# Split operand tiles and right-hand pools on multiples of 64 bytes in a hybrid DeltaNet / gMLP / MLP step

## The chip, the cores and the metric

The kernel runs on one core of a Trainium2 chip. The metric is the device time of one execution in microseconds. A core has a tensor engine (PE, with its weight loads shown apart as PEld), a vector engine (DVE), a scalar engine (ACT), GpSimd (POOL) and a sync engine (SP) whose queue issues the transfers here. Tiles live in SBUF, 128 partitions; a tile's address is a byte offset that is the same in every partition.

## The reference

One layer of a backbone is computed for 128 context tokens and 2048 latent tokens, width 1024. Per token tile:

```
h = rmsnorm(x) * (1 + sc1) + sh1
q, k, v, gate, ab, u, vg = split(h @ w_in)           # q, k, v through a 3-wide convolution and silu
o_a = gated DeltaNet of q, k, v, both directions, chunks of 64, 4 heads x 128
o_b = gelu(u) * (spatial mix of layernorm(gelu(vg)) in chunks of 128)
x = x + ga1 * (concat(rmsnorm(o_a) * silu(gate), o_b) @ w_out)
h = rmsnorm(x) * (1 + sc2) + sh2
x = x + ga2 * (square(relu(h @ w_ff1)) @ w_ff2)       # width 4096
y = rmsnorm(x)
```

The outputs are y of both sequences and the context's final DeltaNet states.

## The kernel before

Every large product is made of three products of operands split into a high and a low part: `mm3` (L213) issues high x high (L217), high x low (L218) and low x high (L219) into the same PSUM tile. The high part is a tile of type fp32r, the low part what is left. Tokens stand in 17 tiles of 128.

*First phase.* Six blocks (`BLOCKS`, L28), five of three token tiles and one of two, are normalised and modulated. `column(k)` (L448) makes the split operands of slice k of the width: `kH` and `kL`, two tiles of 388 columns of 4 bytes from the tag `h`, 24 buffers in the pool `p1`. Block 0 uses 388 columns of them, blocks 1 to 4 use 386 (384 and a neighbour at each end), the last 258. They are streamed through PE (`pj<-kH,wH` and its like): 12 feature tiles (4 each of k, q and v) of 8 slices for each block. At the ends stand single columns, which POOL copies in, zeros from `zcol`.

*Scan.* Then come 34 units of the DeltaNet scan, one for each token tile and direction, beside the gate, gMLP and output projections. A unit prepares a triangular inverse in 16-bit tiles (`AH`, `X`, `Y`, `R` and others) and 32-bit ones (`KK`, `E`, `Es`), which lie in the pool `prep` at the right side of SBUF. When the last unit is prepared, `swap_right` (L1329) closes that pool and opens `hopA` in its place.

*MLP.* Both matmuls use a scheme of seven block products in place of eight (`ORDER`, L54). What PE streams here is a `hop` tile: 4 slices of K, a high and a low part of 512 columns each, 16384 bytes per partition.

```
side, bufs = ("A", 2) if n else ("B", 5)                      # hop_tile, L893
hop[g, o] = t = hop_tile(F32R, o in ORDER[:2])                # first matmul, L900
moved.append(hop_tile(F32R, (len(tcount) - 1) % 5 < 2))       # second matmul, L1630
```

In the first matmul the hop tiles hold the token operands of the seven products for one of two groups of tokens; products 1 and 5 (the first two of `ORDER`) take a tile of `hopA`, the others one of `hopB`. A unit is a pair of 128 columns of the first weight; there are 16 units for each group, and for each product of a unit the four slices of the hop tile are used once: 12 products on PE. In the second matmul the hop tiles hold the second weight, four tiles for each of the seven products, in turn two from `hopA` and three from `hopB`. Its loop (L1757 to the end) runs over `(product, u, q)`: 9 or 8 units u for each product (9, 8, 8, 9, 9, 8, 9), and for each four visits q, one on each hop tile, 12 products each.

*Addresses.* A pool on the left side follows those opened before it, one with `side="right"` grows down from the right end. Tiles are rounded up to 32 bytes. The right end here is byte 229344, 32 more than a multiple of 64. So before the change `hopA` has its two tiles at bytes 196576 and 212960, and all tiles of `prep` lie 32 above a multiple of 64. The five tiles of `hopB` lie on multiples of 64 (from 113024 to 178560), and so do the 49 tiles of `wp`, where the weights and z operands lie. The buffers of `kH` and `kL` are 1568 bytes apart, so every second one is 32 off. A column gives its `kH` and its `kL` neighbouring buffers, so one of the two is off and the other not.

The order of the instructions is set by a scheduler when the program is built, from the order written and dependences. The step from the first phase to the scan reuses addresses: the right pool `prep` takes those where the first phase's `cv`, `x2`, `tk` and `kTt` (pool `p1f`) lay.

Of the kernel before, what the change touches and what calls it, by code (L numbers as in the profile page):

```python
# [8 lines left out]
F32 = mybir.dt.float32  # L9
F32R = mybir.dt.float32r  # L10
# [7 lines left out]
P = 128  # L18
D = 1024
KT = D // P  # L20
# [41 lines left out]
def hybrid_step(  # L62
# [11 lines left out]
    def xrow(t):  # L74
        return x_prompt[0] if t == 0 else x_sample[0, (t - 1) * P : t * P, :]
# [7 lines left out]
    def f32(ap):  # L83
        return ap.bitcast(F32)

    cp = ctx.enter_context(tc.tile_pool(name="const", bufs=1))
    dp = ctx.enter_context(tc.tile_pool(name="dram", bufs=1, space=DRAM))


# [23 lines left out]
    make_identity(nc, ident)  # L113
    ident16 = cp.tile([P, P], F16, name="ident16")
    V.tensor_copy(ident16, ident)
    nhalf = cp.tile([P, 72], F32, name="nhalf")
    V.memset(nhalf, -0.5)
    zcol = cp.tile([P, KT], F32, name="zcol")
    V.memset(zcol, 0.0)
    bd2 = cp.tile([P, P], F16, name="bd2")  # L120
    om = {w: cp.tile([P, P], F16, name=f"om{w}") for w in (2, 4, 8, 16, 32)}
# [50 lines left out]
    def rsqrt_cols(out, ss, n, scale, eps):  # L172
        t = smp.tile([P, 72], F32, tag="rsq", name="rsq", bufs=2)
        np_ = ss.shape[0]
        V.tensor_scalar(out=t[:np_, :n], in0=ss, scalar1=scale, scalar2=eps, op0=ALU.mult, op1=ALU.add)  # L175
        G.tensor_tensor(out=out, in0=t[:np_, :n], in1=nhalf[:np_, :n], op=ALU.pow)  # L176
# [83 lines left out]
    with ExitStack() as ph:  # L260
        p1 = ph.enter_context(tc.tile_pool(name="p1", bufs=2, reuse_waits="tile"))
# [7 lines left out]
        def pt():  # L269
            return ppt.tile([P, 512], F32, tag="pt", name="pt", bufs=3)  # L270
# [121 lines left out]
        def prep_block(bi):  # L392

            tiles = BLOCKS[bi]
            n = len(tiles) * P
            if bi == 0:
                ncol, segs = 388, [(1, 0, P, 0), (131, P, 2 * P, 1)]
            else:
                ncol, segs = n + 2, [(1, 0, n, 1)]
            hH, hL = [], []  # L400
            c0 = tiles[0] * P
            xs = []

            def load_x(t):
                if bi == 0:
                    xs.append(xs0[t])
                    return
                x = p1.tile([P, D], F32, tag="x", name="x", bufs=3)
                load(out=x, in_=xrow(t))
                if t == tiles[0]:  # L410
                    xs.append(smp.tile([P, 3], F32, tag="ss3", name="xss"))
                i = t - tiles[0]
                junk = p1.tile([P, D], BF16, tag="junk", name="junk", bufs=1)
                A.activation(junk, x, AF.Square, accum_out=xs[0][:, i : i + 1])

            def columns_r():
                nt = len(tiles)
                r = smp.tile([P, 3], F32, tag="rk", name="xr")
                rsqrt_cols(r[:, :nt], xs[0][:, :nt], nt, 1.0 / D, EPS)
                diag = p1.tile([P, 3, P], F32, tag="diag", name="diag", bufs=1)  # L420
                V.tensor_tensor(out=diag[:, :nt, :], in0=ident.unsqueeze(1).to_broadcast([P, nt, P]),
                                in1=r[:, :nt].unsqueeze(2).to_broadcast([P, nt, P]), op=ALU.mult)
                xs.append(diag)

            def rows_r():

                pr = pt()
                T.matmul(pr[:, :n], ones, xs[1][:, : len(tiles), :].rearrange("p a b -> p (a b)"), start=True,
                         stop=True)
                xs[1] = p1.tile([P, 384], F32, tag="rrow", name="rrow", bufs=1)  # L430
                A.copy(xs[1][:, :n], pr[:, :n])

            pairs = []

            def load_pair(j):
                x = p1.tile([P, D], F32, tag="x", name="xT", bufs=3)
                x = x[:, : 2 * n].rearrange("p (k t) -> p k t", k=2)
                load(out=x, in_=x_columns.rearrange("(k p) t -> p k t", p=P)[:, 2 * j : 2 * j + 2, c0 - P : c0 - P + n])
                pairs.append(x)

            zc, hc = [], []
            if bi == 0:
                zc, hc = [0, 129, 130], [(387, 1)]
            elif bi == 5:
                zc, hc = [n + 1], [(0, 8)]
            else:
                hc = [(0, 2 * bi - 2), (n + 1, 2 * bi + 1)]
            def column(k):  # L448
                full = p1.tile([P, 384], F32, tag="full", name="full", bufs=2)
                kH = p1.tile([P, 388], F32R, tag="h", name="kH", bufs=24)  # L450
                kL = p1.tile([P, 388], F32R, tag="h", name="kL", bufs=24)
                for col in zc:
                    G.tensor_copy(kH[:, col : col + 1], zcol[:, 0:1])
                    G.tensor_copy(kL[:, col : col + 1], zcol[:, 0:1])
                for col, j in hc:
                    G.tensor_copy(kH[:, col : col + 1], f32(halH)[:, k, j : j + 1])
                    G.tensor_copy(kL[:, col : col + 1], f32(halL)[:, k, j : j + 1])
                if bi == 0:
                    ps = pt()
                    for i, x in enumerate(xs):  # L460
                        T.transpose(ps[:, i * P : (i + 1) * P], x[:, k * P : (k + 1) * P], ident)
                    for s, o, m, cd in segs:
                        A.activation(full[:, o : o + m], ps[:, o : o + m], AF.Identity,
                                     scale=a1[:, cd, k : k + 1], bias=b1[:, cd, k : k + 1])
                    for s, o, m, _ in segs:
                        V.tensor_copy(kH[:, s : s + m], full[:, o : o + m])  # L466
                        V.tensor_tensor(out=kL[:, s : s + m], in0=full[:, o : o + m], in1=f32(kH)[:, s : s + m],
                                        op=ALU.subtract)
                else:
                    if k == 2:  # L470
                        load_pair(3)
                    b = b1[:, 1, k : k + 1]
                    V.scalar_tensor_tensor(out=full[:, :n], in0=pairs[k // 2][:, k % 2, :], scalar=a1[:, 1, k : k + 1],
                                           in1=xs[1][:, :n], op0=ALU.mult, op1=ALU.mult)
                    A.activation(kH[:, 1 : n + 1], full[:, :n], AF.Identity, bias=b)
                    V.scalar_tensor_tensor(out=kL[:, 1 : n + 1], in0=full[:, :n], scalar=b,
                                           in1=f32(kH)[:, 1 : n + 1], op0=ALU.add, op1=ALU.subtract)
                for s, o, m, _ in segs:
                    store(out=hH_d[:, k, c0 + o : c0 + o + m], in_=f32(kH)[:, s : s + m])
                    store(out=hL_d[:, k, c0 + o : c0 + o + m], in_=f32(kL)[:, s : s + m])  # L480
                hH.append(kH)
                hL.append(kL)
            blk = (hH, hL, ncol, segs)
            first = [lambda t=t: load_x(t) for t in tiles]
            if bi:
                first += [lambda: (columns_r(), load_pair(0)), lambda: (rows_r(), load_pair(1)), lambda: load_pair(2)]
            return blk, first, [lambda k=k: column(k) for k in range(KT)]

        def feature_tile(blk, bi, gi, h):
# [249 lines left out]
        side = []  # L739
        for bi in range(len(BLOCKS)):  # L740
# [8 lines left out]
            for n, (gi, h) in enumerate(order):  # L749
# [40 lines left out]
                side = []  # L790
# [114 lines left out]
    with ExitStack() as ph:  # L905
        right = ctx.enter_context(ExitStack())
# [945 lines left out]
    for m, (n, i, u, q) in enumerate(todo):  # L1852
# [12 lines left out]
        h, lo = sops.pop(m)  # L1865
# [72 lines left out]
```

## Time and profile before

| What | Value |
|---|---|
| runs | 2718.88, 2714.51, 2715.29 us; median 2715.29 |
| span of the profiled execution, first to last instruction | 2715.6 us |
| its own time beside the span | not given apart from the runs; the span is 0.3 us over the median |
| granted clock of PE | 0.990 of full speed, mean |
| PE busy | 2631.7 us, 97% |
| DVE, ACT, POOL busy | 1867.8, 1247.8, 226.4 us |
| HBM read, written | 398.14, 179.74 MB |

PE's rows are read by their starts: products overlap in the engine, and the end of each is modelled, so that the time from one start to the next says how fast they follow each other. In a row of the timeline stand start, duration, engine, line, operation, what is written, what is read (the streamed operand first, the stationary one behind it), rows x columns of the stationary operand, and the shape streamed. The names carry no buffer numbers: which hop tile a row reads follows from its place in the loop.

### The profile page before, as it was taken

The page shows a single profiled execution, that of the slowest core. Times are in us where ns is not written, and L with a number is a line of the kernel's source. Part 1 is how long each engine was busy: PE and PEld are TensorE (multiplying, and loading weights), DVE is VectorE, ACT ScalarE, POOL GpSimd, SP SyncE. Part 2 cuts the span into 40 slices and gives each one's busy share as a digit, 9 for nine tenths or more (in the row PEclk, how much of TensorE's full clock was granted, in tenths as well). Part 3 has the DMA queues.
Part 4 walks back from the last instruction along what each step waited for, and adds up shares of the span by engine and source line. Part 5 has one row for each costly group of instructions (what it writes and reads, how often), then busy time and mean ns, then how long its engine had stood idle before and what let it go on. Part 6 is the DMA issues. An engine that isn't in the chain of part 4 may idle for free.

```text
span 2715.6 us, 45142 instructions
## 1 busy us (share of the span) xinstructions
PE 2631.7 (97%) x15682; PEld 2195.9 (81%) x15682; DVE 1867.8 (69%) x3911; ACT 1247.8 (46%) x3092; POOL 226.4 (8%) x448
## 2 busy tenths in 40 slices
PE   8999999999999999899999999999999999999998
PEld 4999998787887777778888778888888787788887
DVE  5867655877777879885677857665565556775874
ACT  4655555555555567763355533332342432332441
POOL 3112113111111111110000000000000000000000
PEclk9999999999999989999999999999999999999999
DMA  8867539555555657885877796333459978776782
GB/s 293 281 198 223 184 119 293 170 159 152 165 160 167 196 174 244 276 271 179 286 222 231 212 311 206 111 110 106 122 166 364 336 257 300 272 240 215 231 262 90
DMA packets 569387, 580.91 MB, mean 214 GB/s; under 512 B 35692, under 2 KB 401692, under 8 KB 565574
## 3 DMA queue, kind: packets, MB, share of 16 engines
q1 hardware_dynamic: 569158, 578.03, 66.9%
q8 instruction: 123, 2.02, 0.3%
q14 instruction: 106, 0.87, 0.1%
HBM read 398.14 MB, written 179.74 MB: 213 GB/s over the span
## 4 chain that ended last, share of the span: by engine, by line
PE 82%; DMA 7%; DVE 6%; issue 2%; ACT 1%; SPq 1%; POOL 0%; DVEq 0%; POOLq 0%; ACTq 0%
PE f L219 16%; PE f L217 16%; PE f L218 16%; PE pj L217 6%; PE pj L219 6%; PE pj L218 6%; PE pd L952 2%; DMA qT<-qT_d 2%; PE pm L217 1%; PE pm L219 1%; PE pm L218 1%; PE pd L1131 1%; DMA raw<-in_w_mod_dram 1%; PE pd L1132 1%; PE pt L568 1%
## 5 line engine op out<-in xcount | busy, mean ns | idle before, releaser
L219 PE MATMUL f<-hop,zL 128*128 128x512 f32 x960 | 377.6, 394 | 1.7 <-DVE zL L1450 1.7
L217 PE MATMUL f<-hop,zH 128*128 128x512 f32 x960 | 377.4, 393 | 1.7 <-ACT zH L1456 1.7
L218 PE MATMUL f<-hop,zH 128*128 128x512 f32 x960 | 377.5, 394 | 0.0
L217 PE MATMUL f<-hop,wH 128*128 128x512 f32 x896 | 356.2, 398 | 6.1 <-ACT wH L1456 6.1
L218 PE MATMUL f<-hop,wH 128*128 128x512 f32 x896 | 352.2, 393 | 0.0
L219 PE MATMUL f<-hop,wL 128*128 128x512 f32 x896 | 352.1, 394 | 0.0
L1456 ACT CAST zH<-zraw 128x512 fp32r<-128x512 f32 x240 | 147.0, 620 | 291.3 <-DVE zraw L1450 90.8
L217 PEld LDWEIGHTS f<-hop,zH 128*128 128x128 f32 x960 | 180.6, 188 | 45.4 <-ACT zH L1456 3.4
L219 PEld LDWEIGHTS f<-hop,zL 128*128 128x128 f32 x960 | 180.7, 188 | 45.0 <-DVE zL L1450 3.5
L218 PEld LDWEIGHTS f<-hop,zH 128*128 128x128 f32 x960 | 180.7, 188 | 41.1
L1450 DVE TENSOR_TENSOR zL<-zraw,zH 128x512 fp32r<-128x512 f32 x240 | 162.6, 686 | 67.9 <-ACT zH L1456 52.6
L217 PEld LDWEIGHTS f<-hop,wH 128*128 128x128 f32 x896 | 169.6, 189 | 41.3 <-ACT wH L1456 6.5
L219 PEld LDWEIGHTS f<-hop,wL 128*128 128x128 f32 x896 | 169.2, 189 | 38.1 <-DVE wL L1450 0.3
L218 PEld LDWEIGHTS f<-hop,wH 128*128 128x128 f32 x896 | 169.4, 189 | 35.4
L217 PE MATMUL pj<-kH,wH 128*128 128x386 f32 (+2 forms) x568 | 190.6, 338 | 0.6 <-DVE kH L466 0.3
L219 PE MATMUL pj<-kH,wL 128*128 128x386 f32 (+2 forms) x568 | 190.3, 335 | 0.0
L218 PE MATMUL pj<-kL,wH 128*128 128x386 f32 (+2 forms) x568 | 189.5, 334 | 0.0
L176 POOL TENSOR_TENSOR r<-rsq,nhalf 128x1 f32<-128x1 f32 (+1 forms) x38 | 23.1, 607 | 1520.8 <-DVE rsq L175 1520.8
L516 DVE SCALAR_TENSOR_TENSOR cv<-pj,vec,cv 128x384 f32<-128x384 f32 (+2 forms) x164 | 87.1, 539 | 60.4 <-ACT cv L513 56.5
L1450 DVE TENSOR_TENSOR wL<-raw,wH 128x512 fp32r<-128x512 f32 x112 | 76.1, 687 | 76.3 <-ACT wH L1456 75.3
L217 PEld LDWEIGHTS pj<-kH,wH 128*128 128x128 f32 x568 | 107.2, 189 | 5.2 <-issue 4.7
L218 PEld LDWEIGHTS pj<-kL,wH 128*128 128x128 f32 x568 | 107.5, 189 | 0.5
(404 smaller groups left out, 6083.0 us busy)
## 6 DMA issues: line engine op xcount, KB each, us to landing
zraw<-z_d SPq DMA_DIRECT2D x212, 256.0 KB
raw<-in_w_ff_dram SPq DMA_DIRECT2D x128, 256.0 KB
hop<-hop_d SPq DMA_DIRECT2D x28, 1024.0 KB
z_d<-c SPq DMA_DIRECT2D x96, 256.0 KB
zraw<-s_d SPq DMA_DIRECT2D x96, 256.0 KB
raw<-in_w_mod_dram SPq DMA_DIRECT2D x80, 256.0 KB
r<-in_w_ff_dram SPq DMA_DIRECT2D x80, 256.0 KB
s_d<-s SPq DMA_DIRECT2D x64, 256.0 KB
```

What stands on the lines that cost most here:

```text
L176: G.tensor_tensor(out=out, in0=t[:np_, :n], in1=nhalf[:np_, :n], op=ALU.pow)
L217: T.matmul(ps, lh, rh, start=first and i == 0, stop=False, skip_group_check=more)
L218: T.matmul(ps, lh, rl, start=False, stop=False, skip_group_check=more)
L219: T.matmul(ps, ll, rh, start=False, stop=last and i == n - 1, skip_group_check=more)
L516: V.scalar_tensor_tensor(out=cv[:, o : o + m], in0=ps[:, s + sh : s + sh + m], scalar=convw[:, w, j : j + 1], in1=cv[:, o : o + m], op0=AL ...
L568: T.matmul(ps[:, i * P : (i + 1) * P], kTt[:, i * P : (i + 1) * P], rhs[:, i * P : (i + 1) * P], start=True, stop=True)
L952: T.matmul(p[:, h, :], lhs[:, h, :], rhs[:, h, :], start=True, stop=True)
L1131: T.matmul(p[:, h, :], u["qT"][:, h, :], s[:, h, :], start=True, stop=False)
L1132: T.matmul(p[:, h, :], u["QK"][:, h, :], u["vn"][:, h, :], start=s is None, stop=True)
L1450: V.tensor_tensor(out=out, in0=a, in1=b, op=op)
L1456: A.copy(h, src)
```

## The change

A pool `edge` is opened first at the right side, and `zcol` (32 bytes) moves into it, so that everything else at the right side lies 32 bytes lower. `nhalf` grows by the 32 bytes that `zcol` leaves free, so the tiles behind both keep their addresses. `kH` and `kL` get 400 columns, a stride of 1600 bytes; the columns that are used stay the same. Afterwards `hopA` lies at bytes 196544 and 212928, the tiles of `prep` on multiples of 64, all 24 buffers of `kH` and `kL` too; what lies above them in `p1` and `p1f` is 768 bytes higher than before.

```
     cp = ctx.enter_context(tc.tile_pool(name="const", bufs=1))
+    edge = ctx.enter_context(tc.tile_pool(name="edge", bufs=1, side="right"))
...
-    nhalf = cp.tile([P, 72], F32, name="nhalf")
+    nhalf = cp.tile([P, 80], F32, name="nhalf")
     V.memset(nhalf, -0.5)
-    zcol = cp.tile([P, KT], F32, name="zcol")
+    zcol = edge.tile([P, KT], F32, name="zcol")
...
-                kH = p1.tile([P, 388], F32R, tag="h", name="kH", bufs=24)
-                kL = p1.tile([P, 388], F32R, tag="h", name="kL", bufs=24)
+                kH = p1.tile([P, 400], F32R, tag="h", name="kH", bufs=24)
+                kL = p1.tile([P, 400], F32R, tag="h", name="kL", bufs=24)
```

The instructions of every engine and their order are the same before and after.

## The prediction

> **What bounds the kernel now.** I read the page's busy times, clock row and chain first, then the costliest groups, then the timeline of PE (the tensor engine), because a change of addresses can act only through the time of single instructions.
>
> ```profile
> span 2715.6 us, 45142 instructions
> PE 2631.7 (97%) x15682; PEld 2195.9 (81%) x15682; DVE 1867.8 (69%) x3911; ACT 1247.8 (46%) x3092; POOL 226.4 (8%) x448
> PEclk9999999999999989999999999999999999999999
> PE 82%; DMA 7%; DVE 6%; issue 2%; ACT 1%; SPq 1%; POOL 0%; DVEq 0%; POOLq 0%; ACTq 0%
> L219 PE MATMUL f<-hop,zL 128*128 128x512 f32 x960 | 377.6, 394 | 1.7 <-DVE zL L1450 1.7
> L217 PE MATMUL f<-hop,wH 128*128 128x512 f32 x896 | 356.2, 398 | 6.1 <-ACT wH L1456 6.1
> ```
>
> PE is busy for 97% of the span and 82% of the chain that ended last. The two last rows stand for the MLP: its 5568 products (3 x 960 + 3 x 896) stream a `hop` tile of 512 columns and wait for other engines for some us in all. So what changes the spacing of PE's instructions changes the time. The mean of 394 to 398 ns is a modelled duration and mixes all tiles; the spacing must be read from starts.
>
> The built programs before and after have the same instructions in the same order on every engine; only addresses and a few waits where the scan follows the first phase differ. Before, the right end of SBUF lies 32 bytes off a multiple of 64, so the two `hopA` tiles start at bytes 196576 and 212960 of a partition, both 32 above a multiple of 64; the five `hopB` tiles start on multiples of 64. In the second matmul of the MLP a visit is 12 products (four slices of K, three products each) on one hop tile, and four visits make one unit. In its first product the tiles of the visits are A, A, B, B. PE's timeline, each row the first L217 of a visit (start, duration):
>
> ```profile
> 2043.16 0.40 PE L217 MATMUL f<-hop,zH 128*128 128x512 f32 x1
> ...
> 2045.97 0.39 PE L217 MATMUL f<-hop,zH 128*128 128x512 f32 x1
> ...
> 2048.77 0.40 PE L217 MATMUL f<-hop,zH 128*128 128x512 f32 x1
> ...
> 2051.53 0.39 PE L217 MATMUL f<-hop,zH 128*128 128x512 f32 x1
> ...
> 2054.25 0.40 PE L217 MATMUL f<-hop,zH 128*128 128x512 f32 x1
> ```
>
> The two A visits take 2.81 and 2.80 us, the B visit after them 2.76, the second B visit 2.72, and no row between has an idle time. 2.72 / 12 = 226.7 ns per product on B, 2.80 / 12 = 233.3 on A. An A visit costs 0.08 to 0.09 us more, and the B visit behind it another 0.04 until the spacing has settled.
>
> **The change part by part.** No edit has a time of its own: `nhalf` has 8 more columns in the one memset that fills it at the start; the pool `edge` holds only `zcol`; `kH` and `kL` are allocated 400 wide, but every instruction on them keeps its 258, 386 or 388 columns. What they bring is addresses: `hopA` and the scan's preparation tiles (same right side) move down by 32 bytes onto multiples of 64, and the split tiles of the first phase, every second of which lay 32 off (stride 1568 bytes, now 1600), all lie on multiples of 64.
>
> *The hop tiles.* Count of A visits: the first matmul has 32 units (16 column pairs, two groups of tokens) and A holds the operands of products 1 and 5: 64 visits. In the second, tile k of the running count is A when k mod 5 is 0 or 1: two visits of four in the products of 9, 8, 8, 8 and 9 units, one in those of 9 and 9, so 2 x 42 + 18 = 102. Together 166 visits, 1992 products. If A runs like B, 166 x 0.085 = 14.1 us go. The after-effect: 60 units of the second matmul x 0.04 = 2.4 us; in the first some 30 more places, but there single products of the context tile lie between and restart the pattern anyway, so I take half, 0.6. Sum 17.1 us; ends 0 (the alignment is not what makes A slow) and 14.9 + 2.4 + 1.2 = 18.5 (0.09 for each visit).
>
> *The split tiles of the first phase.* Here both kinds alternate in one stretch. Rows of the first phase: from 335.69 four triples with `kH` 32 off and `kL` not (8 of 12 products off), then four with `kL` 32 off and `kH` not (4 of 12 off).
>
> ```profile
> 335.69 0.34 PE L217 MATMUL pj<-kH,wH 128*128 128x386 f32 x1
> ...
> 337.83 0.34 PE L217 MATMUL pj<-kH,wH 128*128 128x386 f32 x1
> ...
> 339.96 0.34 PE L217 MATMUL pj<-kH,wH 128*128 128x386 f32 x1
> ...
> 418.67 0.28 PE L217 MATMUL pj<-kH,wH 128*128 128x258 f32 x1
> ...
> 419.75 0.28 PE L217 MATMUL pj<-kH,wH 128*128 128x258 f32 x1
> ```
>
> 2.14 and 2.13 us per 12. What 12 aligned ones would take no row shows. The last two rows hold 9 products of 258 columns in 1.08 us, 120 ns each; with 226.7 for 512 columns that is 0.42 ns per further column, so 386 columns would take 226.7 - 126 x 0.42 = 173.8 ns and 12 of them 2.085 us. The excess is 0.05 us per 12. There are 12 feature tiles x 8 slices x 5 blocks = 480 triples of 386 or 388 columns, so 120 such groups: 6.0 us at most. The least is 0: the two groups differ by 0.01 us only, the products of 258 columns are two thirds off and show no excess over the line through them, and part of the 0.05 can be the ripple behind the transposes that cut in every few products. I take the middle, 3.0 us. PE has nothing else to wait for there:
>
> ```profile
> core 0: us, PE busy (x) PEld busy (x) DVE busy (x) ACT busy (x) POOL busy (x), PEclk, DMA share, GB/s
> 200.00:400.00 200.00, 200.00 (x1233) 190.40 (x1232) 127.97 (x250) 105.83 (x328) 33.94 (x96) 1.00 0.56 174
> 800.00:1000.00 200.00, 182.29 (x1538) 149.00 (x1537) 156.49 (x434) 112.24 (x312) 27.03 (x33) 0.95 0.58 178
> 2040.00:2143.00 103.00, 101.81 (x440) 82.23 (x439) 59.36 (x90) 36.71 (x64) 0.00 (x0) 1.00 0.99 355
> 2143.00:2232.00 89.00, 89.00 (x387) 72.37 (x386) 40.93 (x63) 33.50 (x58) 0.00 (x0) 1.00 0.86 299
> ```
>
> *What takes some back.* DMA, 0.99 busy at 355 GB/s from 2040 to 2143 (the product that also builds the sums of the weights). Nine units there would gain 9 x 0.21 = 1.9 us; if the transfers cannot come faster, PE waits instead. I take 1.0 lost, ends 0 and 1.9. From 2143 on the share is 0.86 and less, DVE 40.93 of 89 us: nobody is late there for a 1% faster PE. If one is, it is the split of z (`zH`, then `zL`), which PE waits on for 1.7 us in all now.
>
> *The scan's preparation tiles.* I cost their move at nothing, from rows of both kinds of address (before the change `R`, `X` and `E` are 32 off; `ident16`, `QK`, `x` and `tmp` are not):
>
> ```profile
> L1084 PE MATMUL pd<-R,X 128*128 128x128 f16 x136 | 13.3, 220 | 0.0
> L1003 PE MATMUL pd<-ident,X 128*128 128x128 f16 x136 | 13.5, 223 | 0.0
> L1044 DVE TENSOR_TENSOR QK<-QK,E 128x512 f32<-128x512 f32 x34 | 23.3, 687 | 19.3 <-DMA QK<-qk_d 12.6 <-POOL E L982 5.4 <-DMA gate_d<-th 1.2
> L1319 DVE TENSOR_TENSOR x<-x,tmp 128x512 f32<-128x512 f32 x34 | 23.3, 686 | 0.5
> ```
>
> A 16-bit product that streams `R` takes 220 ns, one that streams `ident16` 223; DVE with `E` 687, without 686. The stage has slack as well (PE 182.29 of 200).
>
> *The waits where the scan begins.* With the pool edges moved by 768 bytes below and 32 above, the first two units' `KK` and `E` wait for other last users of the phase before; the first load of `KK` waits for one store less, the next load of `hL` for one more. In the chain there:
>
> ```profile
> 447.31 5.14 DMA vt_d<-tk
> ...
> 464.97 2.85 POOL KK L992
> ```
>
> I cost it at 0 with ends of 2.85 us either way, one such step.
>
> Sum: 17.1 + 3.0 - 1.0 = 19.1 us. Against the profiled execution's span, 2715.6 - 19.1 = 2696.5. The median of the three runs is 2715.29, 0.3 less, so I say 2696. From the ends of the terms: least gain with the mechanism right 13.3 + 2.4 + 0 - 1.9 - 2.85 = 11.0 (166 x 0.08 = 13.3), most 18.5 + 6.0 + 2.85 = 27.4.
>
> **The rivals.** *A is slow for another reason than its 32 bytes.* `hopA` is also the highest part of SBUF, and the after-effect shows in aligned B tiles, so place and alignment are not told apart by the MLP's rows. Then `hopA` stays at 2.80, at most the first phase gains, and the time is 2715.6 - 3.0 = 2712.6, no change that can be told. For it: no run has an A tile on a multiple of 64. Against it: 6.7 ns more per product on every A product, in both matmuls of the MLP, is what a fixed number of extra columns at the start or end of a stream would cost (0.42 ns per column: 16 columns, 64 bytes), as an extra piece read per stream would; and `R` above lies higher still, at byte 228320, without a price, though as a 16-bit stream it needs half the bytes.
>
> The Trainium skill bears on this rival: SBUF — State Buffer, section "Door 1: The DMA port swizzle", says that SBUF is read in lines of 16 bytes and that a price comes with each crossing to a new line. By that rule a row of 2048 bytes that starts at a multiple of 32 covers the same 128 lines wherever it starts, no term above would be there, and the time would stay 2715.6. The trace has 2.80 against 2.72 us for rows of the same length, which that rule does not give, but its tiles differ in place as well.
>
> *DMA eats half.* If the weight and z streams set the pace in more than one product, about half of the second matmul's 102 visits come to nothing: 102 x 0.085 / 2 = 4.3, and half of its after-effect, 1.2; 2696.5 + 5.5 = 2702. For it the 0.99 row, against it the 89.00 of 89.00 us busy in the row below.
>
> *Slower.* Before, the preparation tiles and the scan's own tiles lie on different halves of 64 bytes; if equal halves make engines block each other, each of the scan's 170 levels (34 units, five levels: 680 products in groups of four) gets longer on its way PE, DVE, PE. To turn 19 us of gain into more than 5 us of loss the 170 levels must lengthen by 24.5 / 170 = 0.14 us each; with 0.18 it gives 2696.5 + 30.6 = 2727. Against it: the DVE rows above, 687 with tiles on both halves, 686 on one.
>
> **How the numbers follow.** 0.2% is 5.4 us, about what a measurement of this kernel can tell from no change. Forecast (A runs like B) 0.78, DMA takes half 0.07, A slow by place 0.12, slower 0.03. So faster 0.85, same 0.12, slower 0.03. The forecast's own range is 2688 (most gain, 27.4) to 2704.6 (least, 11.0). A range for 8 in 10 reaches from 2688 over both first cases and a part of the third, to 2710.
>
> **What would show it.** Right: four equal visits of 2.72 us per unit in the second matmul; 12 products of 386 columns in 2.09 to 2.11 us; the 16-bit rows and DVE rows as above; the MLP shorter by 16 us and the first phase by 3. Wrong: A visits still of 2.80 (the place, not the alignment); A visits of 2.72 but new idle time of PE before L217 for `zH` (DMA or the split); a first POOL `KK` later than 464.97 less the first phase's gain; longer scan levels.

## The result, and the profile after

| Kernel | runs | median us | lowest to highest | ratio to before, 95% interval |
|---|---|---|---|---|
| before, beside it | 5 | 2715.29 | 2712.76 to 2718.88 | |
| changed | 5 | 2705.08 | 2703.27 to 2710.52 | 0.9962 [0.9951, 0.9974] |

The change makes the kernel 10.2 us faster, by the interval 7.1 to 13.3. That is about half of the 19.1 us that the prediction summed up. The profiled execution of the changed kernel was the slowest of its five (2710.52 us), so its profile shows a smaller gain, 6.9 us of span. In all kernels from here on the three products stand one line lower: L218, L219 and L220. The page of the changed kernel, in the places that were quoted before:

```profile
span 2708.8 us, 45143 instructions
PE 2625.1 (97%) x15682; PEld 2196.0 (81%) x15682; DVE 1867.8 (69%) x3911; ACT 1246.7 (46%) x3092; POOL 226.4 (8%) x448
PE 79%; DMA 8%; DVE 8%; ACT 2%; issue 2%; SPq 1%; POOL 0%; DVEq 0%; POOLq 0%; ACTq 0%
L220 PE MATMUL f<-hop,zL 128*128 128x512 f32 x960 | 377.0, 393 | 1.8 <-DVE zL L1451 1.7
L218 PE MATMUL f<-hop,wH 128*128 128x512 f32 x896 | 356.0, 398 | 7.0 <-ACT wH L1457 7.0
```

PE is 6.6 us less busy, DVE and POOL are as before, and the waits ahead of the products are within 1 us of the old ones: the gain is spacing of products. The mean of one product in the rows shown (393 and 398 ns, before 394 and 398) hardly shows it, as the prediction warned. Its size is in the starts of the visits, on PE's timeline in the same unit of the second matmul (visits A, A, B, B, and the next unit's A):

```profile
2038.58 0.40 PE L218 MATMUL f<-hop,zH 128*128 128x512 f32 x1
...
2041.34 0.40 PE L218 MATMUL f<-hop,zH 128*128 128x512 f32 x1
...
2044.09 0.40 PE L218 MATMUL f<-hop,zH 128*128 128x512 f32 x1
...
2046.86 0.39 PE L218 MATMUL f<-hop,zH 128*128 128x512 f32 x1
...
2049.58 0.40 PE L218 MATMUL f<-hop,zH 128*128 128x512 f32 x1
```

2.76, 2.75, 2.77 and 2.72 us, where before stood 2.81, 2.80, 2.76 and 2.72. The unit is 11.00 us long and was 11.09. A visits became faster, but they did not become like B, and the first B visit behind them even lost 0.01.

The second matmul by stretches, in the windows of before and then of the changed kernel: its first product, the second and third together, and the fourth.

```profile
2032.03:2133.61 101.58, 100.39 (x435) 81.04 (x435) 55.00 (x84) 34.42 (x60) 0.00 (x0) 1.00 1.00 354
2133.61:2313.35 179.74, 179.74 (x774) 144.33 (x773) 101.33 (x158) 58.31 (x100) 0.00 (x0) 1.00 0.86 291
2313.35:2419.09 105.74, 103.47 (x437) 82.12 (x436) 75.45 (x123) 33.04 (x57) 0.00 (x0) 0.98 0.74 247
```

```profile
2027.55:2129.22 101.67, 100.05 (x435) 80.92 (x434) 54.78 (x84) 34.35 (x60) 0.00 (x0) 1.00 0.99 351
2129.22:2307.43 178.21, 178.21 (x774) 144.41 (x772) 100.54 (x156) 57.26 (x98) 0.00 (x0) 1.00 0.85 291
2307.43:2414.21 106.78, 103.86 (x438) 81.51 (x436) 76.83 (x125) 34.43 (x59) 0.00 (x0) 0.98 0.75 250
```

The first numbers are the stretch, its length and PE's busy time; the last three are PE's clock, the share of the DMA engines and GB/s. Where PE is busy all the time (the middle row), 16 units got 1.53 us shorter. In the first product PE's busy time fell by 0.34 us and its length did not: the idle time grew from 1.19 to 1.62 us, with the DMA engines at 0.99. In the fourth both PE's busy time and its idle time are larger than before.

From first to last start, the first matmul went from 727.03 to 724.31 us (-2.7), the second from 674.54 to 672.15 (-2.4), the first phase from 391.1 to 391.5 (+0.4) and the stretch between the two, which holds the scan, from 869.2 to 869.3 (+0.1). Over the 14 profiles of this case the first phase scatters from 391.1 to 394.9 us and the scan's stretch from 864.6 to 870.8, so that one profile does not show a change of 1 us there. The 2.3 us that remain lie ahead of the first phase's first product. That first stretch is 43.2 us long in the profile of before, 43.3 in that of `cols386` (below) and 40.0 to 41.7 in all others. `cols386` and `cols384` have the addresses of before, and `cols384` has 40.4, so nothing ties this length to the change.

### The profile page after: what moved, and what is told of

It reads as the page before. It is cut to its first block, busy times and chain, and to the rows that moved or that the text cites. A ratio compares the mean times of both kernels' runs of the same rounds, so it can differ in the third digit from the quotient of the medians.

```text
span 2708.8 us, 45143 instructions
## 1 busy us (share of the span) xinstructions
PE 2625.1 (97%) x15682; PEld 2196.0 (81%) x15682; DVE 1867.8 (69%) x3911; ACT 1246.7 (46%) x3092; POOL 226.4 (8%) x448
## 3 DMA queue, kind: packets, MB, share of 16 engines
HBM read 398.14 MB, written 179.74 MB: 213 GB/s over the span
## 4 chain that ended last, share of the span: by engine, by line
PE 79%; DMA 8%; DVE 8%; ACT 2%; issue 2%; SPq 1%; POOL 0%; DVEq 0%; POOLq 0%; ACTq 0%
PE f L218 16%; PE f L220 16%; PE f L219 15%; PE pj L218 6%; PE pj L220 5%; PE pj L219 5%; PE pd L953 2%; DMA qT<-qT_d 1%; PE pm L218 1%; PE pm L315 1%; PE pm L219 1%; PE pm L220 1%; DMA QK<-qk_d 1%; PE pd L1132 1%; PE pt L569 1%
## 5 line engine op out<-in xcount | busy, mean ns | idle before, releaser
L218 PE MATMUL f<-hop,zH 128*128 128x512 f32 x960 | 378.2, 394 | 2.7 <-ACT zH L1457 2.7
L220 PE MATMUL f<-hop,zL 128*128 128x512 f32 x960 | 377.0, 393 | 1.8 <-DVE zL L1451 1.7
L219 PE MATMUL f<-hop,zH 128*128 128x512 f32 x960 | 374.4, 390 | 0.0
L218 PE MATMUL f<-hop,wH 128*128 128x512 f32 x896 | 356.0, 398 | 7.0 <-ACT wH L1457 7.0
L220 PE MATMUL f<-hop,wL 128*128 128x512 f32 x896 | 351.3, 393 | 0.0
L219 PE MATMUL f<-hop,wH 128*128 128x512 f32 x896 | 351.1, 392 | 0.0
L220 PEld LDWEIGHTS f<-hop,zL 128*128 128x128 f32 x960 | 180.6, 188 | 46.6 <-DVE zL L1451 5.1
L218 PEld LDWEIGHTS f<-hop,zH 128*128 128x128 f32 x960 | 180.6, 188 | 43.3 <-ACT zH L1457 5.2
L219 PEld LDWEIGHTS f<-hop,zH 128*128 128x128 f32 x960 | 180.7, 188 | 39.4
L218 PEld LDWEIGHTS f<-hop,wH 128*128 128x128 f32 x896 | 169.6, 189 | 40.9 <-ACT wH L1457 7.4
L220 PEld LDWEIGHTS f<-hop,wL 128*128 128x128 f32 x896 | 169.0, 189 | 37.5 <-DVE wL L1451 0.3
L219 PEld LDWEIGHTS f<-hop,wH 128*128 128x128 f32 x896 | 169.5, 189 | 34.0
L218 PE MATMUL pj<-kH,wH 128*128 128x386 f32 (+2 forms) x568 | 190.1, 337 | 0.5 <-DVE kH L467 0.3
L220 PE MATMUL pj<-kH,wL 128*128 128x386 f32 (+2 forms) x568 | 190.3, 335 | 0.0
L219 PE MATMUL pj<-kL,wH 128*128 128x386 f32 (+2 forms) x568 | 189.6, 334 | 0.0
L218 PEld LDWEIGHTS pj<-kH,wH 128*128 128x128 f32 x568 | 107.3, 189 | 5.1 <-issue 4.6
L219 PEld LDWEIGHTS pj<-kL,wH 128*128 128x128 f32 x568 | 107.5, 189 | 0.5
```

Of the source, the lines that this page charges most:

```text
L218: T.matmul(ps, lh, rh, start=first and i == 0, stop=False, skip_group_check=more)
L219: T.matmul(ps, lh, rl, start=False, stop=False, skip_group_check=more)
L220: T.matmul(ps, ll, rh, start=False, stop=last and i == n - 1, skip_group_check=more)
```

## Experiments

"Offset" is from here on a tile's byte address above a multiple of 128. Before, A lay at offset 96 and B at 0; in the changed kernel A lies at 64. `kH` and `kL` lay at 0, 96, 64 and 32 in turn and now lie at 0 and 64 in turn. The stationary operands (`wH`, `wL`, `zH`, `zL`) lie at 0 in both. Diffs are against the changed kernel unless another is named. The theories at the start: what counts is the distance from a multiple of 64 (the prediction's); what counts is the high place in SBUF (its first rival); what counts is the distance from a multiple of 128.

**The two parts alone.** `edge_only` has the pool at the right end and the old width of `kH` and `kL`; `kh_only` is the kernel before with the new width.

```
-                kH = p1.tile([P, 400], F32R, tag="h", name="kH", bufs=24)      # edge_only; kL likewise
+                kH = p1.tile([P, 388], F32R, tag="h", name="kH", bufs=24)
```

> The changed kernel with the first phase's split tiles back at 388 columns (stride 1568 bytes, every second 32 off a multiple of 64); hopA 64 above a multiple of 128 as in the change. Theory 'offset in the MLP alone': the first phase's triples cost the same (530 ns) with either stride, so the time is that of the changed kernel, 2705, within 1 us. Rival 'first phase pays too': its 480 triples lose 4 ns or more in the half with two of three products off, and the time is 2707 or more.

> The kernel before with only the first phase's split tiles at 400 columns; hopA stays 96 above a multiple of 128. Theory 'offset in the MLP alone': 2715, no change; A visits 2.80. Rival 'first phase pays too': 2712 to 2713, the 3 us of the prediction's second term.

`edge_only`: 2710.31 us in 12 runs, ratio 0.9982 [0.9973, 0.9992], 4.9 us less. Its visits are those of the changed kernel (2.76, 2.75, 2.77, 2.72). `kh_only`: 2713.53 us in 12 runs, ratio 0.9997 [0.9986, 1.0007]; its visits are those of before and its first phase is 391.2 us long. By its time, `edge_only` came out where its second theory had it (2707 or more), not within 1 us of 2705; but `kh_only` does not show the 3 us that this theory gives the first phase. Together the two parts give 4.9 + 0.8 = 5.7 us, fewer than the 10.2 and 8.4 (below) of both at once, with intervals that overlap. So the hop tiles bring the gain that the rows show, and of the width of `kH` and `kL` no single comparison shows an effect; that it adds a microsecond or two is not excluded.

**The changed kernel again.**

> The changed kernel once more, beside the others on one chip. Both theories: 2705, some 10 us less than before; A visits 2.75, the B visit behind them 2.77.

2706.6 us in 12 runs, ratio 0.9969 [0.9957, 0.998]: 8.4 us, by the interval 5.4 to 11.7. With the 7.1 to 13.3 of the first runs and the 2.2 to 7.3 of `edge_only`, only some 7 us lies in all three intervals.

**Everything on multiples of 128.** `all128` lets `zcol` take 96 bytes, not 32, so that `hopA` lies at offset 0, and makes `kH` and `kL` 416 columns wide, all at offset 0. `edge128` has the same right end, and 388 columns.

```
-    zcol = edge.tile([P, KT], F32, name="zcol")
+    zcol = edge.tile([P, 24], F32, name="zcol")[:, :KT]
-                kH = p1.tile([P, 400], F32R, tag="h", name="kH", bufs=24)      # kL likewise
+                kH = p1.tile([P, 416], F32R, tag="h", name="kH", bufs=24)
```

> hopA lies on multiples of 128 (bytes 196480 and 212864) and the split tiles of the first phase at a stride of 1664 bytes, also on multiples of 128; nothing else is changed, and the order of the instructions is that of the changed kernel. In the changed kernel hopA lies 64 above a multiple of 128, its visits take 2.75 us (before, 96 above: 2.80), the B visit behind them 2.77, a settled B visit 2.72. Theory 'offset': what counts is the offset within 128 bytes, so A visits and the B visits behind them all take 2.72; the gain over the changed kernel is about 0.12 us in each of 42 units with two A visits, 0.08 in 18 with one and 0.06 in each of the first matmul's 32, together 8 to 9 us, and the time about 2697. Rival 'place': the rest of 0.03 us per A visit belongs to the high end of SBUF: A visits stay at 2.75 and the time at 2705.

> The changed kernel with a pool of 96 bytes in place of 32 at the right end, so that hopA lies on multiples of 128, and with the first phase's split tiles as before the change (388 columns). Theory 'offset in the MLP alone': the time of the kernel with everything on multiples of 128, 2701, 4 to 8 us less than the changed kernel beside it. Rival 'first phase pays too': 2 to 3 us more than that, 2703 to 2704.

`all128`: 2701.31 us, ratio 0.995 [0.9935, 0.9964]. `edge128`: 2700.91 us, ratio 0.9949 [0.9934, 0.9963]. PE's timeline of `all128`, the first A visit, the second and the next unit's first:

```profile
2032.47 0.39 PE L218 MATMUL f<-hop,zH 128*128 128x512 f32 x1
...
2035.19 0.39 PE L218 MATMUL f<-hop,zH 128*128 128x512 f32 x1
...
2043.35 0.39 PE L218 MATMUL f<-hop,zH 128*128 128x512 f32 x1
```

2.72 us for a visit on A and 10.88 for the unit of four: A runs like B and the after-effect is gone, in `edge128` too. The time is 4 us above the 2697 that was expected of `all128`; where the rest stayed is told below (the first matmul, and the first and fourth product of the second). Its windows of the first product and of the second and third together:

```profile
2021.48:2122.09 100.61, 99.27 (x434) 80.76 (x434) 54.84 (x84) 34.27 (x60) 0.00 (x0) 1.00 1.01 357
2122.09:2298.50 176.41, 176.41 (x774) 144.25 (x772) 100.83 (x157) 57.53 (x98) 0.00 (x0) 1.00 0.87 295
```

179.74 before, 178.21 changed, 176.41 here. This is the gain that the prediction had given to multiples of 64.

**A at 32.** `a32` lets `zcol` take 64 bytes: A lies at offset 32.

```
-    zcol = edge.tile([P, KT], F32, name="zcol")
+    zcol = edge.tile([P, 16], F32, name="zcol")[:, :KT]
```

> The changed kernel with a pool of 64 bytes at the right end: hopA lies 32 above a multiple of 128. It shows how the price goes with the offset; known are 0: 2.72, 64: 2.75, 96: 2.80 us for an A visit. Theory 'distance from a multiple of 64': 32 and 96 cost the same, 2.80, and the time is that of the kernel before, 2715. Theory 'the price grows with the offset within 128': between 2.72 and 2.75, and the time 2701 to 2705.

2713.18 us, ratio 0.9992 [0.9977, 1.0006]. Two of its rows, the start of the second A visit and of the B visit behind it:

```profile
2047.28 0.39 PE L218 MATMUL f<-hop,zH 128*128 128x512 f32 x1
...
2050.08 0.40 PE L218 MATMUL f<-hop,zH 128*128 128x512 f32 x1
```

2.80 us, as at 96. So the price does not grow with the distance from a multiple of 128: 0 has none, 64 has 0.03 us per visit, 32 and 96 have 0.08.

**B moved in place of A.** `b96` is `all128` with a 96-byte tile below `hopB`: B at offset 96 and in the lower part of SBUF, A at 0 and on top.

```
+    V.memset(ctx.enter_context(tc.tile_pool(name="shift", bufs=1)).tile([P, 24], F32, name="shift"), 0.0)
     hops["B"] = ctx.enter_context(tc.tile_pool(name="hopB", bufs=1, reuse_waits="tile"))
```

> As the kernel with everything on multiples of 128, but a 96-byte tile below hopB moves its five tiles to 96 above a multiple of 128, at their low place in SBUF; hopA stays on multiples of 128 at its high place. Theory 'offset': the parts change sides: B visits 2.80, A visits 2.72 when settled; 298 B visits x 0.08 = 24 us more than with everything on 128, about 2721. Rival 'place': B visits stay at 2.72 and the time at that of the kernel with everything on 128.

2720.65 us, ratio 1.003 [1.0016, 1.0044], slower than before. The visits B, B, A, A and the next B:

```profile
2039.35 0.40 PE L218 MATMUL f<-hop,zH 128*128 128x512 f32 x1
...
2042.16 0.39 PE L218 MATMUL f<-hop,zH 128*128 128x512 f32 x1
...
2044.96 0.40 PE L218 MATMUL f<-hop,zH 128*128 128x512 f32 x1
...
2047.72 0.39 PE L218 MATMUL f<-hop,zH 128*128 128x512 f32 x1
...
2050.44 0.40 PE L218 MATMUL f<-hop,zH 128*128 128x512 f32 x1
```

2.81, 2.80, 2.76 and 2.72: the pattern of before with A and B exchanged. The high place costs nothing, and the rival of the place falls.

**The split tiles at their worst.** `kh96` is `all128` with a 96-byte tile ahead of `kH` and `kL` in their pool, so that all of them lie at 96; the other tiles of that pool move with them.

```
+        V.memset(p1.tile([P, 24], F32, tag="shift", name="shift", bufs=1), 0.0)
         ones = p1.tile([P, P], F32, tag="ones", name="ones", bufs=1)
```

> As the kernel with everything on multiples of 128, but a 96-byte tile ahead of the first phase's tiles puts all of kH and kL 96 above a multiple of 128 (every tile of that pool, no other product of the MLP). The suspected cost of the first phase is made as large as it gets: three of three products of each triple are off. Theory 'a stream of 386 columns pays like one of 512': 20 ns for each of 480 triples, 9.6 us more than with everything on 128, about 2711. Theory 'these streams pay little or the phase absorbs it': 0 to 3 us more, 2701 to 2704, and triples of 386 columns stay below 536 ns.

2703.47 us, ratio 0.9957 [0.9941, 0.9972]; it is not told apart from `all128`. The eight triples of which the prediction showed the rows of before (335.69 to 339.96, 4.27 us): first and last start in `all128`, then in `kh96`.

```profile
333.81 0.34 PE L218 MATMUL pj<-kH,wH 128*128 128x386 f32 x1
...
338.04 0.34 PE L218 MATMUL pj<-kH,wH 128*128 128x386 f32 x1
```

```profile
334.30 0.34 PE L218 MATMUL pj<-kH,wH 128*128 128x386 f32 x1
...
338.57 0.34 PE L218 MATMUL pj<-kH,wH 128*128 128x386 f32 x1
```

4.23 against 4.27 us. The mean over the 184 triples of 386 columns that stand in undisturbed rows is 527.8 ns in `all128` and 532.3 in `kh96`. For 480 triples the worst offset costs 480 x 4.5 ns = 2.2 us against the best, less than the 3.0 that the prediction expected from half of the way. In the last block, with streams of 258 columns, the order is another: 46 such triples take 366.3 ns in `all128`, 363.6 in `kh96`, 361.9 before and 357.2 in the changed kernel, so there the best offset of the longer streams is the slowest.

**What a shorter stream pays.** `cols386` and `cols384` are the kernel before with three of four visits in the second matmul cut to 386 or 384 columns (the first visit of a unit stays at 512); the other columns of these products are left out.

```
-                mm3(ps, [(h[:, kp, :], lo[:, kp, :], t[:, 0, :], t[:, 1, :])
+                w_ = 512 if q == 0 else 386
+                mm3(ps[:, :w_], [(h[:, kp, :], lo[:, kp, :], t[:, 0, :w_], t[:, 1, :w_])
```

> The kernel before (hopA 96 above a multiple of 128), in whose second matmul the products of the visits q = 1, 2 and 3 use only the first 386 of 512 columns, as wide as the first phase's streams; the other columns of these products are left out. It tells why the first phase did not pay. A 386-column row of 1544 bytes touches 25 pieces of 64 bytes from a multiple of 64 and also 25 from 32 above one; a 512-column row touches 32 and 33. Theory 'one extra piece read': A visits and settled B visits of 386 columns take the same, 2.09 us. Theory 'a fixed price per stream': A visits cost 0.08 more than B visits.

> The same with 384 columns (1536 bytes): 24 pieces of 64 bytes from a multiple of 64, 25 from 32 above. Theory 'one extra piece read': the price is back, B visits 2.08 us when settled and A visits 2.16. Theory 'a fixed price per stream': also 0.08. Theory 'short streams pay less, whatever their end': A visits near B visits in both.

Each has one run. The starts of the visits A, B, B and of the next unit, in `cols386` and then in `cols384`:

```profile
2042.44 0.34 PE L218 MATMUL f<-hop,zH 128*128 128x386 f32 x1
...
2044.60 0.34 PE L218 MATMUL f<-hop,zH 128*128 128x386 f32 x1
...
2046.71 0.34 PE L218 MATMUL f<-hop,zH 128*128 128x386 f32 x1
...
2048.83 0.39 PE L218 MATMUL f<-hop,zH 128*128 128x512 f32 x1
```

```profile
2041.39 0.34 PE L218 MATMUL f<-hop,zH 128*128 128x384 f32 x1
...
2043.51 0.34 PE L218 MATMUL f<-hop,zH 128*128 128x384 f32 x1
...
2045.62 0.33 PE L218 MATMUL f<-hop,zH 128*128 128x384 f32 x1
...
2047.70 0.39 PE L218 MATMUL f<-hop,zH 128*128 128x512 f32 x1
```

With 386 columns A takes 2.16 and the second B 2.12 us; with 384, 2.12 and 2.08. Offset 96 costs 0.04 us per 12 products at both lengths, half of the 0.08 at 512. So it is neither a fixed price per stream nor one that comes and goes with the last two columns. And 12 aligned products of 386 columns take 2.12 us, not the 2.085 that the prediction drew from a straight line: the two columns beyond 384 cost 0.04 us per 12, 3.3 ns per product, where the line from 384 to 512 has 0.64 / 12 / 128 = 0.42 ns per column.

**Whose offset: the stream's or the pair's?** `left64` is `all128` with a 64-byte tile among the constants. Everything on the left lies at offset 64 then: B, the stationary operands and `kH`, `kL`; A stays at 0. `both64` is the changed kernel with that tile and 416 columns: A, B, the stationary operands, `kH` and `kL` all lie at 64.

```
+    V.memset(cp.tile([P, 16], F32, name="shift"), 0.0)
     bd2 = cp.tile([P, P], F16, name="bd2")
```

> As the kernel with everything on multiples of 128, but a 64-byte tile among the constants moves all that lies at the left side up by 64: hopB, the weights and z operands that PE loads as stationary, the first phase's tiles. hopA stays on multiples of 128. Theory 'the stream's own address counts': B visits 2.75 (64 above a multiple of 128), A visits 2.72 when settled, the stationary operand's address without effect. Rival 'what counts is how the stream lies to the stationary operand': both are 64 off for B, so B visits 2.72, and A visits 2.75.

> Everything on the left (hop tiles of B, wp with the stationary operands, kH and kL) and hopA lie 64 bytes above a multiple of 128. If it is the difference between the streamed and the stationary operand's place within 128 bytes that counts, A and B visits both take 2.72 us, no after-effect is left, and the time is that of the version with all on multiples of 128, about 2701 (ratio 0.995). If it is the streamed tile's own place, A and B both take 2.75 as A did in the changed kernel: 1992 products that gain 4.4 ns and about 3580 that lose 2.2 ns against before, about 2714 (ratio 0.9997).

`left64`: 2712.71 us, ratio 0.9987 [0.9974, 1.0001]. Its visits, A, A and the first B:

```profile
2036.10 0.39 PE L218 MATMUL f<-hop,zH 128*128 128x512 f32 x1
...
2038.90 0.39 PE L218 MATMUL f<-hop,zH 128*128 128x512 f32 x1
...
2041.70 0.39 PE L218 MATMUL f<-hop,zH 128*128 128x512 f32 x1
...
2044.44 0.39 PE L218 MATMUL f<-hop,zH 128*128 128x512 f32 x1
```

A, on a multiple of 128, takes 2.80 us, as slow as at 96 before, where 2.75 had been expected of the pair; the second B visit, at 64, takes 2.72. `both64`: 2697.84 us in 5 runs, ratio 0.9935 [0.9921, 0.9949], the lowest median here. Its unit from A to the next A, and its second and third product:

```profile
2035.91 0.39 PE L218 MATMUL f<-hop,zH 128*128 128x512 f32 x1
...
2046.79 0.39 PE L218 MATMUL f<-hop,zH 128*128 128x512 f32 x1
```

```profile
2126.45:2302.86 176.41, 176.41 (x773) 144.24 (x772) 101.49 (x159) 58.62 (x100) 0.00 (x0) 1.00 0.87 297
```

10.88 and 176.41 us, those of `all128`. No operand of the MLP's products lies on a multiple of 128 here, and an undisturbed visit takes 2.72 on A and on B. So what counts is where the streamed tile lies against the stationary operand, not where either lies alone. `left64` moves everything at the left side, and that it acts through the stationary operands is inferred: they are the only other tiles that a product reads.

By which number of bytes the two places are to be compared is not settled. In every kernel where a hop tile runs at 2.72 us, it and the stationary operands share their place within 512 bytes too (both 384 above a multiple of 512 in `all128`, both 448 above in `both64`). And 128 alone does not give the price: a stream 64 above and one 64 below its stationary operand lie alike by 128, but cost 0.03 and 0.08 us. Shorter streams say something on it. In the first phase of `all128` `kH` lies 0, 128, 256 or 384 bytes above the place of `wH` within 512, and the mean triple of 386 columns takes 528.5, 526.6, 527.5 and 528.7 ns (39 to 52 triples each), against 532.3 with all at 96 in `kh96`: there a distance of 128 or 256 costs nothing. For 512 columns none was run.

`all128`, `edge128` and `both64` (intervals 0.9921 to 0.9964) are not told apart, and each has a lower median than both kernels; that of `both64` lies below the changed kernel's 0.9951 to 0.9974 with its whole interval.

Settled visits of 512 columns, 12 products:

| stream at | stationary at | us | ns per product | kernel |
|---|---|---|---|---|
| 0 | 0 | 2.72 | 226.7 | `all128`, B before |
| 64 | 64 | 2.72 | 226.7 | `both64`, B in `left64` |
| 64 | 0 | 2.746 | 228.8 | changed |
| 32 | 0 | 2.80 | 233.3 | `a32` |
| 96 | 0 | 2.80 | 233.3 | A before, B in `b96` |
| 0 | 64 | 2.80 | 233.3 | A in `left64` |

## Why the prediction was right, and where it was not

*What bounds the kernel: right.* The MLP's products follow each other without idle time and got closer together; nothing else became faster by an amount that the times show. Nothing in the runs speaks against "a change of addresses can act only through the time of single instructions".

*"If A runs like B, 166 x 0.085 = 14.1 us go": the step that failed.* Its count, its 0.085 and its after-effect were right, its condition was not. The prediction read addresses by multiples of 64, because A was 32 off and B was not, and took a multiple of 64 for enough. By multiples of 128 A was 96 off and was moved to 64 off, with the stationary operands at 0, and there an A visit takes 2.76 or 2.75 us, not 2.72. The rows of before fit both readings, and the argument of "16 columns, 64 bytes" chose between them without a row that could tell them apart. The five products of the second matmul that wait for no transfer (33 units with two A visits, 9 with one) show it best. By the prediction's terms they gain 33 x (0.17 + 0.04) + 9 x (0.085 + 0.04) = 8.1 us. With offset 0 they went from 467.22 to 459.06 us, 8.2. In the changed kernel they took 463.70, 3.5.

*The after-effect (2.4 + 0.6): did not go.* The B visit behind A was 2.76 and became 2.77 us. It goes only where the spacing is the same on both tiles.

*The first matmul.* 64 x 0.085 + 0.6 = 6.0 us by the terms; 2.7 measured (1.2 and 1.8 in the two other profiles with A at 64), 4.6 in `all128`, 3.4 in `both64` and 4.1 in `edge128`. Even with equal offsets a quarter or more of it was not seen; what cut it there was not tried.

*The first phase, 3.0 us: nothing that the times show.* The floor of 2.085 us per 12 was a straight line through 258 and 512 columns, and 386 columns lie above that line even with equal offsets: 2.12 us (`cols386`), where the two columns beyond 384 have a price of their own. That the products of 258 columns show no excess over a line that goes through them was no evidence. The spacing did get shorter: in `kh_only`, as in the changed kernel, the mean triple of 386 columns went from 532.2 ns (530.4 with one product of three off, 102 triples, and 534.5 with two, 82) to 530.2 or 530.3. That is 480 x 2.0 ns = 1.0 us, too little for the phase's own length to show (391.1, now 391.5, in `kh_only` 391.2). Half of the tiles still lie at 64.

*DMA takes back 1.0 us (0 to 1.9): about right, in one more place than named.* The first and the fourth product of the second matmul should have become 1.2 us shorter by their visits (9 x 0.09 with two A visits, 9 x 0.04 with one). Together they took 1.1 us more in the changed kernel and 0.9 and 1.0 less in the two others with A at 64, so 0.2 to 2.3 was lost. In `all128`, `both64` and `edge128`, where their visits were worth 3.1, they gave 2.2, 0.7 and -0.2, and -0.7 in `kh96`. The prediction looked at the first alone. It also gave PE's wait for the split of z as 1.7 us in all; it is 1.7 for `zL` and 1.7 more for `zH`.

*Costed at nothing.* The scan's rows did not move, and its POOL `KK` came earlier by 1.8 us, like everything since the start. Two groups of instructions and one row of POOL's timeline:

```profile
L1045 DVE TENSOR_TENSOR QK<-QK,E 128x512 f32<-128x512 f32 x34 | 23.4, 687 | 18.9 <-DMA QK<-qk_d 12.5 <-POOL E L983 5.1 <-DMA gate_d<-th 1.2
L1085 PE MATMUL pd<-R,X 128*128 128x128 f16 x136 | 13.3, 221 | 0.0
```

```profile
463.17 2.83 POOL L993 TENSOR_SCALAR_AFFINE_SELECT KK<-KK 128x512 f32<-128x512 f32 x1 [1.00 <-DMA gb<-eg_d]
```

687 ns and 221 ns, before 687 and 220, the POOL step 2.83 us and before 2.85. The row of `R` can't show a price, though: `R` and `X` lie in the same pool, so their places against each other never changed. The products of `ident16` (a constant) with `X` can, since `X` moved from 96 to 64: they take 223 ns as before and start 56 ns apart (median) before, in the changed kernel and in `all128`, where `X` lies at 0. So the price is not seen on these 16-bit products or on DVE's reads here.

*The rivals.* "A is slow by place" fell with `b96`. "Slower" did not come: the scan's stretch is within 0.2 us. What came was in none of the cases: half of the effect. The measured 2705.08 lies in the range given, 2688 to 2710, but 0.5 us outside the forecast's own 2688 to 2704.6: it lies inside because the range was drawn wider towards a rival that did not come true. For the mechanism that is luck; only the direction and the place of the gain came as forecast.

The Trainium skill (SBUF — State Buffer, "Door 1: The DMA port swizzle") gives lines of 16 bytes, by which no offset here would matter. The trace disagrees: the same rows of 2048 bytes, all at multiples of 32, took 2.72, 2.746 or 2.80 us per 12.

*The sum.* With A at 64 three profiles show the MLP 5.1, 5.6 and 6.3 us shorter, the first phase at most 1.0. Some 5 to 7 us are explained by rows. The 10.2 of the first runs lies above that, and the intervals of `after_again` and `edge_only` hold it. Whether the difference is more than the scatter of single runs, 5 to 11 us within most kernels, stays open.

## What to carry to other kernels

Where PE is the bound and streams 32-bit tiles, give the streamed and the stationary tiles the same place; in the fast kernels here they shared it within 512 bytes. It took a padding tile and was worth 14 to 17 us of 2715 by the medians, while "a multiple of 64" gave about half. Closer spacing was shown for streams of 384, 386 and 512 columns, a gain in time for 512 alone; streams of 258 columns did not gain. Read alignment as an address relative to the other operand, and test a rule of alignment with a kernel that moves the other side (`left64`) before believing it. A price per instruction that the profile shows is only as good as the condition under which it goes: run the state that is aimed at before summing it over 2000 instructions.

## What the runs showed of the hardware

- A 32-bit (fp32r) product of 512 columns follows the one before it by 226.7 ns where stream and stationary operand share their place within 512 bytes, by 228.8 to 233.3 where it differs by 32, 64 or 96. It is not symmetric: a stream 64 above the stationary operand's place costs 2.1 ns more, one 64 below it 6.7. Distances of 128 and 256 were free for streams of 386 columns (`all128`) and were not run for 512. Stationary operands at 32 or 96 were not tried, and why the pair counts stays open.
- The first visit (12 products) on a fast tile behind a slow one is still 0.02 to 0.05 us longer than a settled one.
- 12 products at equal offsets take, with 384 columns, 2.08 us, with 386 columns 2.12, with 512 columns 2.72: the two columns beyond 384 cost as much as eight by the slope from 384 to 512.
